# A four-mixer decoder trunk: the attention's value sum in fp32 products, and new constants for the planner that orders the instructions

## The chip, the cores and the metric

The kernel runs on one core of one Trainium2 chip. Time is the device time of one execution in microseconds, and each figure for a kernel is the median of its runs. A profile is one execution in which the hardware recorded every instruction; its span runs from the first instruction to the last.

## The reference

Two layers work on a sequence of 512 positions of width 1024, all in float32. Each layer does this:

```
h = rmsnorm(x);  z = h @ w_in                       # 1024 -> 13 column groups
y_a = a_b * conv3(a_c * a_h)                        # short causal convolution
y_b = g_u * (tril(W_s) @ layernorm(g_v) + b_s)      # per chunk of 128, 4 heads
y_c = attention(q, k, v), 4 heads of 64, rotary; of the admissible keys only the
      128 that score highest in sum_j w_idx_j * relu(q_idx_j . k_idx) take part
y_d = silu(layernorm(conv31(d_a * sigmoid(d_g)) + b))   # conformer, 31 taps
x = x + concat(y_a, y_b, y_c, y_d) @ w_out
x = x + (silu(hf @ w_gate) * (hf @ w_up)) @ w_down,  hf = rmsnorm(x)   # hidden 2816
```

A last rmsnorm closes the trunk.

## The kernel before

**Products.** Activations lie with features on the 128 partitions and the 512 positions along the free dimension. A product of two float32 matrices is made of three fp32r products: each operand is split into a high half, a copy rounded to fp32r (ScalarE, `pg.act`), and a low half, the operand less its high half (`pg.tt` with `subtract`, on VectorE or GpSimd); `mm3` then adds high times high, high times low and low times high in one bank of PSUM. A few small products (sums over partitions, spreading a row over partitions, transposes) use float32 operands directly, which here is called an fp32 product. In the trace an fp32 product shows as two records.

**Weights.** They come in units of 128 x 1024 in the order of use: 23 for the input projections of a layer (`in_units`, the order of whose parts is `ORDER`: c are the conformer's, a the attention's q and k, s the short convolution's, g the gate of the chunked mixer, z the values of both that mixer and the attention), 10 for the output projection, 44 for gate and up, 24 for down. `weights()` loads a unit and splits it; `POOL_LO` names the units whose low half GpSimd computes, `DEEP` those whose halves lie in the large pool of 68 buffers `u` of 128 x 512 (and whose load is gated) and not in the four `wh`/`wl` pairs. While layer 0's gate and up products run, all 33 input and output units of layer 1 are split and stored (`presplit`), and layer 1 loads them as pairs.

**Side chains.** Beside the projections run the rotary products (`rope`), the search for the 128 best keys (`topk`: 16 rounds of MAX8 and MATCH_REPLACE8 for each of three query blocks, on VectorE), the conformer's taps (`conf`: `TAPS` of the 31 on VectorE in a PSUM bank, the rest on ScalarE and GpSimd) and its layer norm (`conf_ln`), the softmax, and the value sum. The value sum, per head and per block `s_` of 128 keys: transposes of the probabilities into a bank `sm`, a split of that bank into `hi` and `lo`, and `mm3` with the halves `vh`, `vl` of the values into the bank `po`, over 512, 384, 256 and 128 columns.

**Output projection.** For each of its eight row blocks first the six groups `EARLY_K`, which are y[0], y[1], y[6], y[7], y[2], y[3], that is all but the attention; the attention's two (`LATE_K`) follow in a second pass.

**Order.** The program is first recorded as operations with their dependencies (`Program.add`). `order` then walks backwards for the latest time at which each may start (projection products, the mains, at nominal times stretched by `STRETCH`; other operations scaled by `HURRY`), subtracts the boost of its part (`BOOST`, one table a layer), and simulates the five engines forwards with a cost for each operation and a model of TensorE's clock (`clock`), always picking the most urgent operation that can start. The order that comes out is what each engine's queue holds. So the constants change no arithmetic, but they can move any instruction on its engine.

**Start.** `warm` puts `WARMUP` fp32 products of a constant at the head of TensorE's queue. The first unit (`HALVED`) is loaded and split in two halves.

## Time and profile before

| | |
|---|---|
| median of 3 runs | 1168.21 us (1168.18 to 1168.29) |
| profiled execution | 1167.96 us |
| its span | 1166.2 us |
| TensorE (PE) busy | 1146.0 us |
| VectorE (DVE) busy | 651.2 us |
| ScalarE (ACT) busy | 486.5 us |
| GpSimd (POOL) busy | 279.4 us |
| mean granted TensorE clock | 0.993 |

A matmul's record lasts longer than its share of the engine, because matmuls are pipelined: the engine's pace is read from the starts of consecutive records, or from a run in the chain of waits. A line number in a row is often that of a helper (L335 is `mm`, L383 `tt`, L392 `stt`, L429 and L431 `act`), so rows are told apart by the names of their tiles: `mm`, `cv`, `sm`, `po` are PSUM banks, `wr`, `wh`, `wl` a unit of weights and its halves, `u` everything in the large pool, `X` the residual stream. PE is TensorE, PEld its weight loads, DVE VectorE, ACT ScalarE, POOL GpSimd. The granted clock is a share of 2.4 GHz, and 0.50 is the lower level of 1.2 GHz.

### The profile page before, as it was taken

The page shows a single profiled execution, that of the slowest core. Times are in us where ns is not written, and L with a number is a line of the kernel's source. Part 1 is how long each engine was busy: PE and PEld are TensorE (multiplying, and loading weights), DVE is VectorE, ACT ScalarE, POOL GpSimd, SP SyncE. Part 2 cuts the span into 40 slices and gives each one's busy share as a digit, 9 for nine tenths or more (in the row PEclk, how much of TensorE's full clock was granted, in tenths as well). Part 3 has the DMA queues.
Part 4 walks back from the last instruction along what each step waited for, and adds up shares of the span by engine and source line. Part 5 has one row for each costly group of instructions (what it writes and reads, how often), then busy time and mean ns, then how long its engine had stood idle before and what let it go on. Part 6 is the DMA issues. An engine that isn't in the chain of part 4 may idle for free.

```text
span 1166.2 us, 14577 instructions
## 1 busy us (share of the span) xinstructions
PE 1146.0 (98%) x5266; PEld 934.1 (80%) x5266; DVE 651.2 (56%) x1169; ACT 486.5 (42%) x803; POOL 279.4 (24%) x213
## 2 busy tenths in 40 slices
PE   9999989999999999999999999999999999999996
PEld 6878768888888888888877787788888888888885
DVE  5799996644346566553236999756433433433212
ACT  7583557533234554442123553655323323332211
POOL 1758822211111111021111664003111111100111
PEclk9999989999999999999999999999999999999998
DMA  9620213232359999994672452232233232234202
GB/s 321 207 82 21 75 41 108 76 115 90 105 172 308 374 361 387 369 367 154 224 239 76 180 186 99 78 127 91 91 95 105 91 101 98 86 106 142 97 5 72
DMA packets 75576, 178.44 MB, mean 153 GB/s; under 512 B 9200, under 2 KB 15472, under 8 KB 75504
## 3 DMA queue, kind: packets, MB, share of 16 engines
q1 hardware_dynamic: 72304, 172.26, 42.8%
q10 hardware_dynamic: 3200, 5.25, 1.3%
q8 instruction: 41, 0.67, 0.2%
q14 instruction: 31, 0.25, 0.1%
HBM read 139.17 MB, written 34.11 MB: 149 GB/s over the span
## 4 chain that ended last, share of the span: by engine, by line
PE 82%; DVE 11%; DMA 2%; ACT 2%; issue 1%; POOL 0%; SPq 0%; DVEq 0%; POOLq 0%; ACTq 0%
PE mm L335 76%; DVE u L950 2%; DVE cv L392 2%; DVE u L383 2%; DVE m L949 2%; PE sm L352 2%; PE sm L335 1%; PE po L335 1%; DMA dr<-u 1%; DMA u<-w_dram 1%; DVE u L392 1%; ACT u L431 1%; PE cv L335 1%; PE sm L361 1%; DVE wl L383 1%
## 5 line engine op out<-in xcount | busy, mean ns | idle before, releaser
L335 PE MATMUL mm<-u,wh 128*128 128x512 f32 (+1 forms) x2548 | 735.9, 391 | 2.3 <-ACT wh L429 0.9
L335 PEld LDWEIGHTS mm<-u,wh 128*128 128x128 f32 (+1 forms) x2548 | 476.2, 187 | 105.0 <-DVE u L392 2.0
L335 PE MATMUL mm<-u,wl 128*128 128x512 f32 (+1 forms) x1274 | 432.3, 391 | 1.4 <-DVE wl L383 1.4
L383 POOL TENSOR_TENSOR u<-u,u 128x512 f32<-128x512 f32 (+10 forms) x174 | 237.5, 1376 | 754.0 <-ACT u L431 626.0
L429 ACT CAST wh<-wr 128x1024 fp32r<-128x1024 f32 (+2 forms) x151 | 152.6, 1016 | 375.2 <-PE mm L335 311.4
L335 PEld LDWEIGHTS mm<-u,wl 128*128 128x128 f32 (+1 forms) x1274 | 238.7, 187 | 52.2 <-DVE wl L383 3.1
L335 PE MATMUL mm<-u,u 128*128 128x512 f32 (+1 forms) x816 | 223.7, 380 | 0.3
L383 DVE TENSOR_TENSOR u<-mm,u 128x512 f32<-128x512 f32 x119 | 81.6, 689 | 232.0 <-PE mm L335 225.0
L383 DVE TENSOR_TENSOR wl<-wr,wh 128x1024 fp32r<-128x1024 f32 (+2 forms) x144 | 169.9, 1186 | 50.1 <-ACT wh L429 49.9
L335 PEld LDWEIGHTS mm<-u,u 128*128 128x128 f32 x816 | 147.6, 189 | 35.0 <-issue 4.2
L383 DVE TENSOR_TENSOR u<-u,u 128x512 fp32r<-128x512 f32 (+3 forms) x150 | 106.6, 734 | 32.6 <-ACT u L429 27.3
L429 ACT CAST u<-u 128x512 fp32r<-128x512 f32 (+2 forms) x148 | 84.6, 590 | 79.9 <-DVE u L383 26.5
L383 DVE TENSOR_TENSOR X<-X,mm 128x512 f32<-128x512 f32 (+1 forms) x49 | 32.9, 675 | 123.9 <-PE mm L335 123.9
L392 DVE SCALAR_TENSOR_TENSOR cv<-u,prm,cv 128x511 f32<-128x511 f32 (+17 forms) x72 | 52.8, 733 | 0.0
L950 DVE MATCH_REPLACE8 u<-m,u 128x256 f32<-128x256 f32 (+2 forms) x96 | 51.7, 541 | 0.0
L949 DVE MAX8 m<-u 128x8 f32<-128x512 f32 (+2 forms) x96 | 51.3, 550 | 0.3
L431 ACT ACTIVATE u<-u 128x512 f32<-128x512 f32 x60 | 37.8, 631 | 18.5 <-DVE u L383 15.5
L431 ACT ACTIVATE u<-X,prm 128x512 fp32r<-128x512 f32 (+1 forms) x39 | 27.4, 717 | 35.0 <-DVE X L383 34.6
L431 ACT ACTIVATE u<-u,prm 128x512 f32<-128x512 f32 (+13 forms) x56 | 35.2, 704 | 9.9 <-POOL u L383 8.8
L392 DVE SCALAR_TENSOR_TENSOR u<-X,prm,u 128x512 fp32r<-128x512 f32 x32 | 27.9, 904 | 11.4 <-ACT u L431 8.8
L431 ACT ACTIVATE u<-X 128x512 f32<-128x512 f32 (+1 forms) x33 | 19.8, 607 | 31.2 <-DVE X L383 27.8
L431 ACT ACT_TABLE_LOAD x18 | 23.1, 1283 | 22.2 <-DVE rc L660 9.8
(96 smaller groups left out, 501.0 us busy)
## 6 DMA issues: line engine op xcount, KB each, us to landing
wr<-w_dram SPq DMA_DIRECT2D x143, 512.0 KB, 3.6
dr<-u SPq DMA_DIRECT2D x114, 256.0 KB, 5.6
u<-w_dram SPq DMA_DIRECT2D x57, 256.0 KB, 5.7
u<-dr SPq DMA_DIRECT2D x56, 256.0 KB, 4.9
wr<-w_dram SPq DMA_DIRECT2D x24, 384.0 KB, 3.0
wh<-dr SPq DMA_DIRECT2D x12, 512.0 KB, 4.5
wl<-dr SPq DMA_DIRECT2D x12, 512.0 KB, 5.8
u<-u ACTq DMA_DIRECT2D x28, 128.0 KB, 2.3
```

The lines of the kernel that those rows point to most:

```text
L335: self.add("PE", cost, lambda: self.nc.tensor.matmul(out.ap(), l.ap(), r.ap(), start=start, stop=stop), [out.tile.view], [l, r], lat=0.2, ...
L352: self.nc.tensor.matmul(o.ap(), a.ap(), b.ap(), start=start, stop=stop)
L361: self.nc.tensor.transpose(o.ap(), x.ap(), ident.ap())
L383: self.add(eng, cost, lambda: self._e(eng).tensor_tensor(out=out.ap(), in0=a.ap(), in1=b.ap(), op=op), [out], [a, b], port=eng == "POOL" o ...
L392: self.add("DVE", 0.13 + 1.0417e-3 * out.n, lambda: self.nc.vector.scalar_tensor_tensor(out=out.ap(), in0=a.ap(), scalar=self._sc(s), in1= ...
L429: self.nc.scalar.copy(out.ap(), x.ap())
L431: self.nc.scalar.activation(out.ap(), x.ap(), func, **{k: self._sc(v) for k, v in kw.items()})
L949: pg.dve(n, lambda m8=m8, sc=sc: nc.vector.max(out=m8.ap(), in_=sc.ap()), [m8], [sc])
L950: pg.dve(n, lambda m8=m8, sc=sc: nc.vector.match_replace(out=sc.ap(), in_to_replace=m8.ap(), in_values=sc.ap(), imm_value=-3e38), [sc], [m8])
```

## The change

The value sum keeps values and probabilities as they are (`WHOLE`, both layers): one copy out of PSUM and one fp32 product a block, in place of a copy, a subtraction and three fp32r products. The conformer's tap counts are looked up by layer. The values of the constants of the order change: the order of the input parts (q1 and k1 ahead of gu1), stretch, boosts, clock model, the cost of a warm-up product and the number of them (12 to 17), the sets `DEEP` and `POOL_LO`, and a boost for the first half of a halved unit's split.

```diff
@@ -31,7 +31,7 @@
     "s0": [("ac", 0), ("ah", 0), ("ab", 0)], "s1": [("ac", 1), ("ah", 1), ("ab", 1)],
     "g0": [("gu", 0)], "g1": [("gu", 1)],
 }
-ORDER = ('z', 'c0', 'a0', 's0', 'c1', 's1', 'g0', 'g1', 'a1')
+ORDER = ('z', 'c0', 'a0', 's0', 'c1', 's1', 'g0', 'a1', 'g1')
 N_IN = 23
 COL = {"qi": QI, "q": Q, "k": K, "da": D_A, "dg": D_G, "ac": A_C, "ah": A_H, "ab": A_B, "gu": G_U}
 DOWN_PARTS = [(0, 8), (8, 16), (16, 22)]
@@ -200,7 +200,7 @@
                 o.key -= FIRST
 
         engs = ["PE", "DVE", "ACT", "POOL", "SP"]
-        self.slow, self.edge, self.busy = 2.0, WINDOW, 0.0
+        self.slow, self.edge, self.busy = 2.0, 2.3, 0.0
         free = dict.fromkeys(engs, 0.6)
         future = {e: [] for e in engs}
         avail = {e: [] for e in engs}
@@ -370,7 +370,7 @@
         def fn():
             for _ in range(n):
                 self.nc.tensor.matmul(out.ap(), x.ap(), x.ap(), start=True, stop=True)
-        self.add("PE", n * (1.667e-3 * out.n + 0.01), fn, [out], [x], lat=0.2)
+        self.add("PE", n * 0.185, fn, [out], [x], lat=0.2)
 
     def _sc(self, s):
         return s.ap() if isinstance(s, View) else s
@@ -465,23 +465,25 @@
 
 
 WINDOW, COOL, WARM = 3.41, 0.42, 0.7
-STRETCH = 1.18
-WARMUP = 12
+STRETCH = 1.09
+WARMUP = 17
 PRESPLIT = 3
+
+WHOLE = (0, 1)
 AHEAD = (80, 220)
-HURRY = 1.07
+HURRY = 1.19
 EARLY = -6.0
-FIRST = 104.0
+FIRST = 100.0
 FIN_POOL = (0, 2)
 
 BOOST = [
-    {"rope": -2.0, "conv": 19.0, "a": 16.0, "z": 6.0, "s": 30.0, "g": -2.0, "topk": 6.0, "att": 30.0, "out": -3.0},
-    {"rope": 2.0, "conv": 26.0, "a": -1.0, "z": -1.0, "s": 10.0, "g": -9.0, "topk": 2.0, "att": 20.0, "out": 6.0},
+    {"rope": -2.0, "conv": 19.0, "a": 16.0, "z": 4.0, "s": 15.0, "g": 4.0, "topk": 12.0, "att": 61.0, "out": -1.0},
+    {"rope": 2.0, "conv": 19.0, "a": -1.0, "z": 10.0, "s": 0.0, "g": 0.0, "topk": 3.0, "att": 2.0, "out": -1.0},
 ]
-DEEP = (2, 4, 5, 6, 7, 9, 10, 11, 12, 13, 15, 20, 23, 25, 26, 28)
+DEEP = (4, 5, 6, 7, 9, 10, 11, 12, 15, 20, 23, 25, 31)
 HALVED = (0,)
-TAPS = (18, 20)
-POOL_LO = (5, 7, 10, 11, 12, 14, 18, 20, 21, 22, 23, 29, 31, 32)
+TAPS = (18, 20, 18, 20)
+POOL_LO = (3, 5, 7, 11, 12, 14, 20, 21, 22, 23, 25, 26, 29, 31)
 
 
 def build(tc, nc, a, o):
@@ -592,7 +594,9 @@
             hi, lo = (pg.tile(t, [128, 1024], F32R)[:, :w] for t in ("wh", "wl"))
             for n, c in enumerate((slice(0, w // 2), slice(w // 2, w))):
                 first_load(raw[:, c], a["w"][i, :, c], 2 + 6 * n)
+                pg.boost += 20.0 * (1 - n)
                 split(raw[:, c], hi[:, c], lo[:, c])
+                pg.boost -= 20.0 * (1 - n)
             return lambda c, n: (hi[:, c:c + n], lo[:, c:c + n])
         sooner = pg.mains[-AHEAD[0]:][:1] if i >= N_UNITS + N_IN + N_OUT else ()
         pg.dma(raw, a["w"][i, :, :w], after=gate if deep else sooner)
@@ -780,7 +784,7 @@
             pg.tt(ar, pa, R, ALU.mult)
             pg.tt(yp, ar, gr, ALU.mult, "POOL")
             w = [pm[:, P_WC + CW * i + d:P_WC + CW * i + d + 1] for d in range(CW)][::-1]
-            cv, cd, nv = pg.tile("cv", [128, S]), U(), TAPS[i]
+            cv, cd, nv = pg.tile("cv", [128, S]), U(), TAPS[2 * l + i]
             pg.act(cv, yp, AF.Identity, scale=w[0], bias=pm[:, P_BC + i:P_BC + i + 1])
             for e in range(1, nv):
                 pg.stt(cv[:, e:], yp[:, :S - e], w[e], cv[:, e:], ALU.mult, ALU.add)
@@ -842,14 +846,17 @@
             gv, vn = [], []
             for t in range(4):
                 if t % 2 == 0:
-                    g2, h2, l2 = U(), U(F32R), U(F32R)
+                    g2, h2 = U(), U(F32 if l in WHOLE else F32R)
+                    l2 = h2 if l in WHOLE else U(F32R)
                 c = slice(256 * (t % 2), 256 * (t % 2) + 256)
                 gv.append(g2[:, c])
                 vh.append(h2[:, c])
                 vl.append(l2[:, c])
                 pg.act(gv[t], pz[t][:, :G])
                 pg.act(vh[t], pz[t][:, G:], AF.Copy, scale=rs[:, t:t + 1])
-                pg.stt(vl[t], pz[t][:, G:], rs[:, t:t + 1], f(vh[t]), ALU.mult, ALU.subtract)
+                if l not in WHOLE:
+                    pg.stt(vl[t], pz[t][:, G:], rs[:, t:t + 1], f(vh[t]), ALU.mult,
+                           ALU.subtract)
 
 
             ws, bl, lbs, wsh, wsl = U(), U(), U(F32R), U(F32R), U(F32R)
@@ -991,6 +998,15 @@
                 pt = SM()[:, :n]
                 pg.trs([pt[:, 128 * (b - s_):128 * (b - s_) + 128] for b in range(s_, 4)],
                        [probs[h, b][:, 128 * s_:128 * s_ + 128] for b in range(s_, 4)], ident)
+                if l in WHOLE:
+                    if s_ < 3:
+                        hi = U()
+                        pts[s_] = hi[:, :n]
+                        if s_ == 1:
+                            pts[3] = hi[:, 384:]
+                    pg.act(pts[s_], pt)
+                    pg.mm(po[:, 128 * s_:], vh[s_][:, c], pts[s_], s_ == 0, s_ == 3)
+                    continue
                 if s_ < 3:
                     hi, lo = U(F32R), U(F32R)
                     pts[s_] = hi[:, :n], lo[:, :n]
```

## Rows read from the trace of the kernel before

**Rows 1.** The page's busy line: us, share of the span, instructions.

```profile
PE 1146.0 (98%) x5266; PEld 934.1 (80%) x5266; DVE 651.2 (56%) x1169; ACT 486.5 (42%) x803; POOL 279.4 (24%) x213
```

**Rows 2.** Stretches: us, busy PE, PEld, DVE, ACT, POOL, clock, DMA share, GB/s.

```profile
0.00:25.00 25.00, 22.56 (x95) 16.50 (x96) 11.02 (x18) 19.16 (x39) 3.62 (x11) 1.00 0.93 338
...
143.00:152.00 9.00, 8.03 (x38) 6.26 (x37) 9.00 (x24) 3.89 (x7) 8.27 (x6) 1.00 0.24 73
152.00:165.00 13.00, 9.51 (x37) 6.84 (x38) 12.73 (x34) 10.44 (x19) 0.55 (x1) 0.74 0.09 31
...
178.00:205.00 27.00, 27.00 (x163) 22.47 (x161) 16.10 (x46) 19.36 (x49) 6.62 (x3) 1.00 0.34 115
...
660.00:719.00 59.00, 58.03 (x262) 46.67 (x260) 57.70 (x134) 22.84 (x42) 34.95 (x32) 1.00 0.53 191
...
775.00:800.00 25.00, 24.54 (x108) 19.94 (x108) 19.41 (x23) 13.41 (x20) 8.95 (x6) 1.00 0.14 46
...
1150.00:1166.00 16.00, 6.07 (x42) 5.30 (x40) 6.55 (x23) 3.55 (x9) 2.82 (x4) 0.71 0.39 131
```

**Rows 3.** Timeline of TensorE, 140 to 206 us: start, us, instruction, idle before it.

```profile
151.17 0.62 PE L335 MATMUL mm<-u,wh 128*128 128x512 f32 x2
155.06 1.16 PE L335 MATMUL sm<-ident,rs 128*128 128x128 f32 x8 [3.26 <-DVE rs L392]
...
157.13 0.80 PE L335 MATMUL mm<-u,wl 128*128 128x512 f32 x1 [0.43 <-DVE wl L383]
```

**Rows 4.** One microsecond of the stretch from 152 to 165, columns as in rows 2.

```profile
157.00:158.00 1.00, 0.87 (x2) 0.78 (x3) 1.00 (x3) 0.29 (x1) 0.00 (x0) 0.50 0.00 0
```

**Rows 5.** The chain that ended last, in order of time: start, us, what.

```profile
25.90 0.89 PE sm L335 x8
...
203.01 1.85 PE po L335 x12
204.87 23.49 PE mm L335 x103
```

**Rows 6.** Timeline of TensorE around the two fp32 products of 512 columns.

```profile
141.50 1.02 PE L335 MATMUL sm<-u,o 128*128 128x512 f32 x2
142.29 0.93 PE L335 MATMUL mm<-u,u 128*128 128x512 f32 x3
...
713.37 1.13 PE L335 MATMUL sm<-u,o 128*128 128x512 f32 x2 [0.59 <-POOL u L383]
...
714.57 0.39 PE L335 MATMUL mm<-u,u 128*128 128x512 f32 x1
```

**Rows 7.** VectorE's groups by shape: count, busy us, mean ns, idle before.

```profile
L383 DVE TENSOR_TENSOR u<-sm,u 128x512 fp32r<-128x512 f32 x8 | 5.2, 687 | 1.5 <-ACT u L429 1.4
...
L383 DVE TENSOR_TENSOR u<-sm,u 128x384 fp32r<-128x384 f32 x8 | 4.3, 547 | 0.2 <-ACT u L429 0.2
...
L383 DVE TENSOR_TENSOR u<-sm,u 128x256 fp32r<-128x256 f32 x8 | 3.4, 419 | 3.3 <-ACT u L429 3.3
...
L392 DVE SCALAR_TENSOR_TENSOR u<-mm,rs,u 128x256 fp32r<-128x256 f32 x6 | 2.7, 480 | 0.5 <-ACT u L429 0.3
...
L383 DVE TENSOR_TENSOR u<-sm,u 128x128 fp32r<-128x128 f32 x8 | 1.9, 281 | 1.0 <-ACT u L429 1.0
```

**Rows 8.** Groups by shape: a unit's low half on VectorE and on GpSimd.

```profile
L383 DVE TENSOR_TENSOR wl<-wr,wh 128x1024 fp32r<-128x1024 f32 x123 | 150.4, 1228 | 19.9 <-ACT wh L429 19.8
...
L383 POOL TENSOR_TENSOR wl<-wr,wh 128x1024 fp32r<-128x1024 f32 x6 | 14.4, 2402 | 16.8 <-ACT wh L429 16.8
```

**Rows 9.** Timeline of VectorE, 196 to 232 us.

```profile
205.52 0.69 DVE L383 TENSOR_TENSOR u<-po,u 64x512 fp32r<-64x512 f32 x1 [3.07 <-ACT u L429]
...
212.45 0.69 DVE L383 TENSOR_TENSOR X<-X,mm 128x512 f32<-128x512 f32 x1 [0.27 <-PE mm L335]
```

**Rows 10.** Timeline of TensorE in the first microseconds.

```profile
1.06 5.49 PE L372 MATMUL mm<-ones 128*128 128x128 f32 x24 [1.06 <-POOL ones L631]
...
7.40 0.73 PE L335 MATMUL mm<-u,wh 128*128 128x512 f32 x2 [0.86 <-ACT wh L429]
```

## Prediction

> **What bounds the kernel now.** I read the page's busy line first. TensorE is busy for 1146.0 of 1166.2 us, VectorE for 651.2 [rows 1]. So a column more on TensorE is paid in full, and all that can be won is TensorE's idle time and slow clock. The idle time is 1166.2 - 1146.0 = 20.2 us, and the stretches say where. The first 25 us hold 25.00 - 22.56 = 2.4 us, the stretch from 1150 to the end 16.2 - 6.07 = 10.1, and neither is in the part that is rewritten, except for the warm-up. That leaves 7.7 us in the middle [rows 1, 2].
>
> Of these, 9.00 - 8.03 = 1.0 and 13.00 - 9.51 = 3.5 us lie between 143 and 165 us, in layer 0's mixers, and there alone the mean granted clock is under 1: 0.74 over 13 us, which is (1 - 0.74) x 13 = 3.4 us of work lost [rows 2]. The timeline shows the event. TensorE starts its last two ready products at 151.17, then idles 3.26 us until VectorE delivers `rs`, the conformer's layer norm scale, at 155.06, and waits once more for a weight's low half from VectorE at 157.13 [rows 3]. After that gap the clock stands at the lower level, 0.50 of full, 1.2 GHz, through the microsecond at 157 and beyond [rows 4]. This one stall costs 1.0 + 3.5 + 3.4 = 7.9 us. The other 7.7 - 4.5 = 3.2 us of idle time are spread; layer 1's counterpart holds 59.00 - 58.03 = 1.0, its entry into the FFN 0.5 [rows 2].
>
> The cause is a queue on VectorE. It is busy 9.00 of 9.00 us before the stall and 12.73 of 13.00 in it [rows 2]: top-k, conformer taps, rotary products and weight splits share it, and TensorE has used up the input projections before the conformer's output exists (the first output unit needs y[6], y[7] as its third and fourth products).
>
> **The change part by part.** *The value sum on TensorE.* Today a head takes twelve fp32r products, and a run of twelve takes 1.85 us [rows 5]. Afterwards it takes four fp32 products over 512 + 384 + 256 + 128 = 1280 columns. Their price is read from fp32 products that are already there. Four of 128 columns (eight records, so two a product) take 0.89 us, 1.74 ns a column [rows 5]. One of 512 columns (two records) starts at 141.50 and the next work at 142.29, 0.79 us; the other starts at 713.37, and after it and one fp32r product (23.49 / 103 = 0.23 us) it is 714.57, so 0.97 [rows 5, 6]. Per column these are 1.54 and 1.89 ns. A head then costs 1280 x 1.74 = 2.22 us (1.97 to 2.42), that is 0.37 more than 1.85 (0.12 to 0.57), and eight heads cost **+2.9 us** (+1.0 to +4.6). I take the middle, because the run of four is the one most like the new sum.
>
> The section "Back-to-back issue gap" of the Trainium skill's page "TensorE: Matmul & The Clock Gate" gives one gap for N columns at full clock, N / 2.4 GHz + 2.5 ns, and makes no exception for fp32. By it a head's four products would take about 0.54 us, an estimate from that page, and the term would be a gain of some 10 us in place of the loss. The eight records of the four small fp32 products contradict it: 0.89 us where the page's gap gives 0.22.
>
> *The splits on VectorE.* The subtractions that make the low halves of the probabilities go: 32 of them, 5.2 + 4.3 + 3.4 + 1.9 = 14.8 us. So do eight of the values' low halves at 0.48, 3.8 us [rows 7]. ScalarE's copies stay, since the high half was a copy of the same shape. So 18.6 us leave an engine that is off the path for most of the span, and only what is queued ahead of something TensorE waits for counts. The 7.4 us a layer of the probabilities fall in the value sums, 178 to 205 us, where VectorE is busy for 16.10 of 27 and TensorE never idle [rows 2]: nothing directly. The values' 1.9 us a layer come before top-k. One wait also goes (a product no longer waits for a subtraction, and the bank of transposes comes free earlier); output products cover it today, so I count nothing; without that cover each block would give back its subtraction, 0.28 to 0.69 us.
>
> *Splits that change engine.* In layer 0, units 10 (k0), 18 (ab1) and 32 go from GpSimd to VectorE, units 3 (z0), 25 and 26 the other way. A 1024-wide one costs 1.23 us on VectorE and 2.40 on GpSimd [rows 8]. Two of those that come to VectorE fall before the stall, +2.4 us against the 1.9 that the values free. In amount, then, VectorE's queue there is not shorter. If the stall goes, it goes by order.
>
> *The order.* What can be moved is top-k and attention. The last value sum's split ends at 205.52 + 0.69 = 206.2, and the first late output group, six products of 0.23 us, ends at 212.45, so starts near 211.1: attention has 4.9 us to spare [rows 5, 9]. The removed subtractions give it up to 7.4 us more. So top-k can make way for the conformer by about ten microseconds, more than the 3.3 + 0.4 us by which the conformer is late [rows 3]. Moving q1 and k1 ahead of gu1 also starts the last two heads one unit sooner. The boosts speak both ways: layer 0's `s` falls from 30 to 15, behind `conv` at 19, but `topk` rises from 6 to 12 and `att` from 30 to 61. `HURRY` rises, which draws long side chains forward, and the conformer's is one. I take most of the stall as gone, with 1.7 us left of 7.9, a little over what layer 1's counterpart still loses: **-6.2** (bounds -7.9 and 0). For the 3.2 us elsewhere, with 9.3 us less on VectorE in each layer, I take **-1.3** (-3.2 to 0).
>
> *The start.* Twelve warm-up products take 5.49 us, 0.46 each, and end at 6.55; the first real product starts at 7.40 [rows 10]. Five more end at about 8.9 at that pace, and at 7.7 at the full-clock 0.22 of the 128-wide fp32 product [rows 5]; so first work slips 0.3 to 1.5 us. Unit z0's low half comes 2.40 - 1.23 = 1.2 us later from GpSimd [rows 8], with unit qi1 now loaded without its gate to fill in. Later waits for data in these 25 us absorb part (2.4 us idle [rows 2]). I take **+0.5** (-0.6, if the earlier first split starts TensorE sooner and hides the rest, to +2.7).
>
> *At nothing.* The tap counts are the same 18 and 20 for both layers. The deep set changes which buffers hold four units' halves; the splits stay as wide in sum and products cover them. Layer 1's input and output weights come split from memory as before; if a pair came late, a wait like the 0.5 us one would appear. The gate, up and down products are untouched, and that stretch has no idle time worth a term.
>
> **Sum.** The profiled execution took 1167.96 us (span 1166.2, 1.8 outside), 0.25 below the median of 1168.21. 1167.96 + 2.9 - 6.2 - 1.3 + 0.5 = 1163.9, and with the 0.25 added, **1164**.
>
> **The rivals.** (A) As above, 0.44: own range 1160.5 to 1165.8.
>
> (B) Every stall goes, as VectorE's queue is shorter and better ordered: 1168.2 + 2.9 - 7.9 - 3.2 = 1160.0. For it: the slack above. Against: VectorE stays full ahead of the stall. 0.13.
>
> (C) The other side. The conformer stays late: two more splits and a top-k that has moved nearer to it keep VectorE's queue as long, TensorE again runs dry near 151 us, and the clock falls again. The price is the unhidden 2.9 of fp32, 0.5 at the start, -1.3 elsewhere: 1168.2 + 2.1 = 1170.3, or 1171.6 with nothing won elsewhere. It decides from the point where less than about 2.9 of the 11.1 us of stalls and slow clock goes. 0.19.
>
> (D) The stall is shortened, not removed: idle without the fall of the clock, or half of it. About 3.4 of 7.9 saved: 1168.2 + 2.9 + 0.5 - 3.4 = 1168.2. 0.17.
>
> (E) The new order makes a second stall of that kind, at the value sums, where TensorE now waits on ScalarE's copies, or in layer 1: 1168.2 + 2.1 + 7.9 = 1178.2. Today's 27.00 of 27.00 busy there [rows 2] speaks against it. 0.05.
>
> (F) An fp32 product costs no more than an fp32r one. A head would take a third of 1.85, eight heads -9.9 in place of +2.9, and the time 1151.3. This is the skill's rule above; the two records a product and 0.89 us [rows 5] speak against it. 0.02.
>
> **How the numbers follow.** About 0.2%, 2.3 us, is what a measurement of this kernel can tell from no change. Faster: A, B and F, 0.59; no change: D, 0.17; slower: C and E, 0.24. The range for 8 in 10 runs from B's low side, 1159, to C's high side, 1171.5; it leaves out E, F and the edges of B and C.
>
> **What would show it.** In the new trace: two long records a product in the value sum, a run of four over 1280 columns at 2.2 us (2.0 to 2.4); no low-half subtraction reading `sm` or scaled by `rs` on VectorE, some 18 us less of its time; TensorE's idle time in the middle down from 7.7 us to about 3, its clock at full through 143 to 165 us; TensorE's time in value sums up by about 3. The prediction is wrong if the clock still falls in layer 0, if the fall only moves to another stage, or if the fp32 sum costs more than 4.6 us because fp32 and fp32r products alternate badly. Then the order, not the arithmetic, is what I misjudged.

## The result, and the profile after

The changed kernel takes 1179.57 us (median of 4 runs, 1177.65 to 1180.32), the kernel before 1168.25 beside it (1168.18 to 1169.81). The ratio is 1.0091, 95% interval 1.0078 to 1.0105: slower by 0.9%. Forecast were 1164.0 us and a range that ended at 1171.5.

The page of the changed kernel (span 1178.5 us, profiled run 1180.32), the line that answers to [rows 1]:

```profile
PE 1149.3 (98%) x5244; PEld 931.1 (79%) x5244; DVE 640.9 (54%) x1125; ACT 484.8 (41%) x798; POOL 272.1 (23%) x214
```

TensorE is busy 3.3 us longer and idle 1178.5 - 1149.3 = 29.2 us in place of 20.2. So most of the loss is waiting. VectorE's busy time is 10.3 us shorter, not 18.6. The low halves of [rows 7] are all gone; what came back is mostly in other splits: there are three more of 1024 columns, and those of 512 take 0.80 us in the mean in place of 0.74.

Stretches of the changed kernel, columns as in [rows 2]:

```profile
0.00:25.00 25.00, 22.18 (x104) 16.65 (x105) 9.85 (x17) 19.40 (x39) 3.96 (x12) 1.00 0.95 340
...
125.00:150.00 25.00, 21.65 (x92) 16.78 (x92) 24.97 (x50) 7.76 (x14) 21.07 (x17) 1.00 0.23 69
150.00:175.00 25.00, 21.63 (x103) 16.39 (x103) 22.29 (x53) 14.25 (x25) 8.16 (x6) 1.00 0.15 49
...
200.00:225.00 25.00, 22.44 (x99) 14.66 (x98) 10.14 (x29) 15.35 (x39) 0.36 (x1) 0.93 0.12 41
...
450.00:475.00 25.00, 22.14 (x91) 17.84 (x90) 13.48 (x19) 11.43 (x17) 3.81 (x3) 0.93 1.02 380
```

The slow clock of [rows 2] and [rows 4] is gone from the stage around 155 us, but it shows in two others, each (1 - 0.93) x 25 = 1.75 us, together 3.5 us, about the 3.4 of before. The idle time, too, lies in more places than it did. The list of what TensorE waited for up to 240 us, so in layer 0's mixers, says how: total us, times, longest us. First the kernel before:

```profile
PE sm L335 <- DVE rs L392: 3.3, 1, 3.3
PE mm L335 <- DVE wl L383: 1.4, 3, 0.8
PE mm L372 <- POOL ones L631: 1.1, 1, 1.1
PE mm L335 <- ACT wh L429: 0.9, 1, 0.9
```

Then the changed kernel:

```profile
PE mm L335 <- DVE wl L383: 3.4, 4, 2.1
PE sm L352 <- DVE u L383: 1.8, 1, 1.8
PE sm L335 <- DVE rs L392: 1.4, 1, 1.4
PE sm L335 <- POOL u L383: 1.2, 1, 1.2
PE mm L335 <- DVE u L383: 1.2, 2, 0.7
PE sm L352 <- DVE mx L403: 1.2, 1, 1.2
PE mm L372 <- POOL ones L635: 1.1, 1, 1.1
PE mm L335 <- ACT u L429: 1.0, 2, 0.7
PE mm L335 <- ACT wh L429: 1.0, 1, 1.0
PE po L335 <- DVE u L383: 0.6, 1, 0.6
PE mm L335 <- DVE u L392: 0.6, 2, 0.3
```

The wait for `rs` did shrink, from 3.3 to 1.4 us. But the sum of the list went from 6.7 to 14.5 us, and in place of six waits it holds seventeen. And one wait came far from there, at 469 us in layer 0's FFN (the feed-forward part: the gate, up and down products). TensorE's timeline of the changed kernel (start, us, instruction, idle before it), around the longest of them:

```profile
57.74 0.73 PE L352 MATMUL sm<-u,u 64*128 64x512 f32 x4 [1.84 <-DVE u L383]
...
149.80 0.50 PE L335 MATMUL mm<-u,wl 128*128 128x512 f32 x1 [2.10 <-DVE wl L383]
...
155.59 1.13 PE L335 MATMUL sm<-ident,rs 128*128 128x128 f32 x8 [1.38 <-DVE rs L392]
...
205.59 0.55 PE L352 MATMUL sm<-u,u 64*128 64x128 f32 x5 [1.16 <-DVE mx L403]
...
465.95 0.39 PE L335 MATMUL mm<-u,wl 128*128 128x512 f32 x1
469.20 0.73 PE L335 MATMUL mm<-u,wh 128*128 128x512 f32 x2 [2.86 <-DVE u L383]
```

Where the time went along the span shows best on TensorE's own work. The program has 4722 projection products in the same number in every kernel here, so I compare the starts of the product with 864 before it (the mixers of layer 0 and its output projection are done), of that with 2160 before it (layer 0's FFN has run on past 469 us), of that with 3312 before it (layer 1's mixers are done), and the end of the span. They are counted from the traces, in us later than in the kernel before:

```
                              865th   2161st   3313th     end
after                        +10.34   +14.36   +12.01  +12.27
fp32_old_order                +1.22    +0.74    -0.26   -0.29
new_order_fp32r               +6.69   +11.89    +9.27   +9.37
old_constants_fp32            +9.63   +10.24    +9.42   +9.35
new_constants_split          +11.41   +13.82   +24.61  +24.93
half_search                   +9.20   +11.62    +9.30   +9.52
pool_halves_new               +8.02   +10.43    +9.18   +9.41
one_store                    +12.28   +16.28   +14.26  +14.46
ffn_eviction_moved            +8.12    +8.47    +6.97   +7.37
waits_moved                   +4.16    +4.35    +1.87   +2.09
half_searches_new             +3.09    +7.11    +4.47   +4.71
stall_moved                   +1.52    +1.95    +2.05   +2.02
half_searches_old             -0.98    -0.71    -0.72   -0.74
chain_moved                   +0.86    +1.77    +1.84   +1.64
chain_and_lows_moved          +5.62    +6.24    +6.44   +5.92
```

So the change loses 10.3 us in layer 0's mixers and 4.0 more in its FFN, and wins 14.36 - 12.01 = 2.35 in layer 1. These are one profiled execution each, and a median can stand some 2 us off it. The table itself shows that: *ffn_eviction_moved* changes nothing ahead of the FFN, and yet its 865th product stands at +8.12 and not at +10.34. Most of the difference is the wait of 1.84 us at 57.74, which it does not have.

Two causes can be read from rows. **A queue.** In the FFN the bank that TensorE wants is evicted by VectorE (`u<-mm`). VectorE's timeline, then ScalarE's:

```profile
467.22 1.23 DVE L383 TENSOR_TENSOR wl<-wr,wh 128x1024 fp32r<-128x1024 f32 x1 [1.71 <-ACT wh L429]
468.37 1.28 DVE L383 TENSOR_TENSOR u<-mm,u 128x512 f32<-128x512 f32 x2
```

```profile
466.15 1.04 ACT L429 CAST wh<-wr 128x1024 fp32r<-128x1024 f32 x1 [1.36 <-PE mm L335]
```

The eviction stands behind the split of a weight that TensorE does not need yet (with the split put behind it, below, the wait shrinks to 0.5 us). That split waits for a cast, and the cast waits for a buffer that TensorE's last products before the stall give back. A free engine, a finished product, and 2.86 us of waiting. **A lock.** VectorE's subtraction of two operands in SBUF, the engines' working memory, takes 1.23 us at 128x1024 [rows 8], and 0.66 at 128x512 where nothing delays it (below). VectorE's timeline of the changed kernel has longer ones:

```profile
54.85 2.84 DVE L383 TENSOR_TENSOR u<-u,u 128x512 fp32r<-128x512 f32 x1
...
147.24 0.54 DVE L957 MATCH_REPLACE8 u<-m,u 128x384 f32<-128x384 f32 x1
147.70 2.05 DVE L383 TENSOR_TENSOR wl<-wr,wh 128x1024 fp32r<-128x1024 f32 x1
```

and GpSimd's has, at those times:

```profile
54.78 2.36 POOL L383 TENSOR_TENSOR wl<-wr,wh 128x1024 fp32r<-128x1024 f32 x1 [3.29 <-ACT wh L429]
...
147.40 1.27 POOL L383 TENSOR_TENSOR u<-u,u 128x512 f32<-128x512 f32 x1 [0.68 <-ACT u L431]
```

In each pair VectorE's instruction outlasts GpSimd's by less than its own length: GpSimd ends at 54.78 + 2.36 = 57.14 and VectorE at 57.69; GpSimd at 148.67 and VectorE at 149.75. TensorE's waits of 1.84 and 2.10 us end within 0.05 us of that. The search step ahead of the second, at 147.24, ran into the same GpSimd instruction and kept its length. That VectorE and GpSimd lock each other out of a shared port pair for a whole instruction, when VectorE reads two SBUF operands, stands in the Trainium skill, "SBUF — State Buffer", section "SBUF: two separate sides"; these rows agree, 2.84 us for 0.66.

Which of the two starts first is not the order's to say. In *ffn_eviction_moved*, whose order up to there is the same to the instruction, the subtraction of 54.85 started before GpSimd's, and TensorE did not wait. VectorE's row, then GpSimd's:

```profile
54.28 0.66 DVE L387 TENSOR_TENSOR u<-u,u 128x512 fp32r<-128x512 f32 x1
```

```profile
54.73 2.47 POOL L387 TENSOR_TENSOR wl<-wr,wh 128x1024 fp32r<-128x1024 f32 x1 [2.23 <-ACT wh L433]
```

Of the six profiled runs with this order there, GpSimd was first in the changed kernel and in *one_store*, and only these two have the wait of 1.8 us.

### The profile page after: what moved, and what is told of

Same layout as the page of the kernel before. It is cut to its first block, busy times and chain, and to the rows that moved or that the text cites. A ratio compares the mean times of both kernels' runs of the same rounds, so it can differ in the third digit from the quotient of the medians.

```text
span 1178.5 us, 14460 instructions
## 1 busy us (share of the span) xinstructions
PE 1149.3 (98%) x5244; PEld 931.1 (79%) x5244; DVE 640.9 (54%) x1125; ACT 484.8 (41%) x798; POOL 272.1 (23%) x214
## 4 chain that ended last, share of the span: by engine, by line
PE 82%; DVE 11%; DMA 2%; ACT 2%; issue 1%; ACTq 0%; POOL 0%; DVEq 0%
PE mm L335 77%; DVE cv L392 3%; DVE u L383 2%; DVE u L957 2%; DVE m L956 2%; PE po L335 2%; PE sm L352 2%; PE sm L335 1%; ACT u L431 1%; PE sm L361 1%; DVE wl L383 1%; DMA u<-u 1%; DVE u L392 1%; DMA wr<-w_dram 1%; DMA X<-x_dram 1%
## 5 line engine op out<-in xcount | busy, mean ns | idle before, releaser
L335 PE MATMUL mm<-u,wh 128*128 128x512 f32 x2628 | 801.1, 392 | 4.9 <-DVE u L383 3.3
L335 PEld LDWEIGHTS mm<-u,wh 128*128 128x128 f32 x2628 | 491.0, 188 | 112.4 <-issue 5.9
L335 PE MATMUL mm<-u,wl 128*128 128x512 f32 x1314 | 488.3, 392 | 3.6 <-DVE wl L383 3.6
L383 POOL TENSOR_TENSOR u<-u,u 128x512 f32<-128x512 f32 (+12 forms) x174 | 229.7, 1332 | 797.4 <-ACT u L431 650.6
L335 PEld LDWEIGHTS mm<-u,wl 128*128 128x128 f32 x1314 | 246.1, 187 | 57.6 <-DVE wl L383 5.8
L335 PE MATMUL mm<-u,u 128*128 128x512 f32 (+1 forms) x696 | 183.1, 373 | 2.2 <-DVE u L383 1.2
L335 PEld LDWEIGHTS mm<-u,u 128*128 128x128 f32 x696 | 125.3, 188 | 28.3 <-DVE u L383 2.2
L383 DVE TENSOR_TENSOR u<-u,u 128x512 fp32r<-128x512 f32 (+2 forms) x150 | 109.6, 747 | 53.2 <-ACT u L429 32.0
L429 ACT CAST u<-u 128x512 fp32r<-128x512 f32 (+1 forms) x148 | 84.9, 590 | 81.8 <-DMA u<-w_dram 31.1
L957 DVE MATCH_REPLACE8 u<-m,u 128x512 f32<-128x512 f32 (+2 forms) x96 | 51.7, 541 | 0.0
L431 ACT ACTIVATE u<-u,prm 128x512 f32<-128x512 f32 (+13 forms) x56 | 34.9, 699 | 11.3 <-POOL u L383 11.2
```

The costliest lines, as they stand in the source:

```text
L335: self.add("PE", cost, lambda: self.nc.tensor.matmul(out.ap(), l.ap(), r.ap(), start=start, stop=stop), [out.tile.view], [l, r], lat=0.2, ...
L383: self.add(eng, cost, lambda: self._e(eng).tensor_tensor(out=out.ap(), in0=a.ap(), in1=b.ap(), op=op), [out], [a, b], port=eng == "POOL" o ...
L429: self.nc.scalar.copy(out.ap(), x.ap())
L431: self.nc.scalar.activation(out.ap(), x.ap(), func, **{k: self._sc(v) for k, v in kw.items()})
L957: pg.dve(n, lambda m8=m8, sc=sc: nc.vector.match_replace(out=sc.ap(), in_to_replace=m8.ap(), in_values=sc.ap(), imm_value=-3e38), [sc], [m8])
```

## Experiments

### Arithmetic and order apart

*fp32_old_order*: the old order to the instruction, with the new sums. The two dropped products and the low halves keep their place in the order and issue nothing.

```diff
+    def sum3(out, lh, rh, first, last):
+        (ah, al), (bh, bl) = lh, rh
+        for n, (x, y_) in enumerate(((ah, bh), (ah, bl), (al, bh))):
+            pg.mm(out, x, y_, first, last)
+            pg.ops[-1].cost = max(0.1, 0.4167e-3 * y_.n + 0.0133)
+            if n:
+                pg.ops[-1].fn = lambda: None
...
-                mm3(po[:, 128 * s_:], (vh[s_][:, c], vl[s_][:, c]), pts[s_], s_ == 0, s_ == 3)
+                pg.ops[-1].fn = lambda: None
+                sum3(po[:, 128 * s_:], (vh[s_][:, c], vl[s_][:, c]), pts[s_], s_ == 0, s_ == 3)
```

> The kernel before with its exact order on every engine; only the value sum is done in fp32 products of unsplit probabilities and values, and the subtractions for their low halves are not issued. Theory O (the loss is in the new order; the arithmetic costs what the small fp32 products showed, 0.37 us a head): 1171 us (1169 to 1172.5), layer 0's attention ends within 2 us of where it ended before (206.2). Theory F (the fp32 products themselves cost far more, by alternating with fp32r products): 1177 or more.

Measured: 1167.9 us (before 1168.38), ratio 0.9996 [0.9987, 1.0006]. That is under Theory O's range by 1 us, and 9 under Theory F's.

*new_order_fp32r*: the new order to the instruction, each fp32 product issued as three fp32r products of the high halves. The low halves are left out.

```diff
-                    pg.mm(po[:, 128 * s_:], vh[s_][:, c], pts[s_], s_ == 0, s_ == 3)
+                    thrice(po[:, 128 * s_:], vh[s_][:, c], pts[s_], s_ == 0, s_ == 3)
```

> The changed kernel with its exact order; each fp32 product of the value sum is replaced by three fp32r products of the high halves (the low halves are left out), no subtraction. Theory O: only the 2.9 us of the arithmetic come back, 1176.5 us (1175 to 1178.5), and layer 0 still falls 8 us or more behind. Theory F: most of the 11 us come back, 1170 or less.

Measured: 1175.95, ratio 1.0062 [1.0047, 1.0077]: Theory O's range, though layer 0 is behind by 6.7 us and not by 8.

*old_constants_fp32*: the new arithmetic, planned anew with all of before's constants and cost figures. Against the kernel before, beside the lines of the new value sum:

```diff
+WHOLE = (0, 1)
...
-TAPS = (18, 20)
+TAPS = (18, 20, 18, 20)
```

> The changed kernel's arithmetic with all constants of the kernel before (order of parts, boosts, sets, stretch, clock and warm-up model), planned anew. Theory O, in the form that the constants are at fault: 1173 or less, with layer 0's search for the best keys ended by 175 us and its attention by 212. Theory O in the form that any change of costs makes the planner's order fall out by several us either way: anywhere from 1168 to 1180, with a new place of the stall. Theory F: 1178 or more.

Measured: 1176.99, ratio 1.0072 [1.0057, 1.0087]: not the 1173 or less of constants at fault, but inside the range of the second form.

*new_constants_split*: the new constants, planned for the old arithmetic (`WHOLE = ()`).

> The changed kernel with the split value sum of the kernel before (three fp32r products, low halves computed), planned anew with the new constants. Theory O, constants at fault: 1177 or more, layer 0 behind by 8 us or more. Theory F: 1170 or less.

Measured: 1193.34, ratio 1.0217 [1.02, 1.0234]. Here 10.8 us of the loss arise in layer 1, by the table.

The first two answer the main question. The arithmetic in the old order costs nothing that can be measured. The new order without the arithmetic is slower by 0.6%. The other two say what kind of thing the order is: neither set of constants is good in itself, since before's constants are as bad for the new arithmetic as the new constants are, and the new constants are much worse for the old arithmetic. A planner that lists some seven thousand instructions by due time gave another order after each of these edits, and the one of before is the best of the four. Why it is, no run shows. Nor was any one constant or set (`DEEP`, `POOL_LO`, the warm-up) put back by itself.

### Three suspects for the new order

*half_search*: in the new order the search of the second query block, which now ends at 192.3 in place of 170.1 us, does 8 of its 16 rounds.

```diff
+                if (l, b) == (0, 1) and rnd >= 8:
+                    for o_ in pg.ops[-2:]:
+                        o_.fn = lambda: None
```

> The changed kernel with its exact order, but layer 0's search for the second query block (256 wide) does 8 of its 16 rounds; the other 8 are left out, some 7 us of VectorE. Theory S (the late search holds back layer 0's attention and that holds back TensorE after 202 us): the search ends near 181 in place of 192.3, the last value sum's split near 211 in place of 221.2, and the time falls by 5 us or more (1174 or less). Rival V (the value sums on TensorE are themselves the chain there): attention ends within 2 us of 221 and the time stays within 2 us of 1179.6.

Measured: 1179.05, ratio 1.0078 [1.0054, 1.0103]. The search ends at 177.3, and the last value sum at 218.8, where it had ended at 219.9. So Rival V: this search's late end is not what holds attention back.

*pool_halves_new* and *pool_halves_old*: GpSimd's wide two-operand instructions issued in two halves, so that the lock is shorter, in the new and in the old order.

```diff
...
+        if eng == "POOL" and out.shadow.ndim == 2 and out.n >= 480:
+            h = out.n // 2
+            parts = [(out[:, c], a[:, c], b[:, c]) for c in (slice(0, h), slice(h, out.n))]
...
```

> The changed kernel with its exact order; GpSimd's tensor operations of 480 columns and more are issued as two halves, so that a colliding VectorE instruction can get in between. Theory K (VectorE loses 16 us up to 165 us, in place of 8 before, to instructions that stand still while GpSimd reads SBUF, and this makes the conformer and the search late): that loss falls by a third or more, layer 0 gains 3 us or more, time 1176.5 or less. Rival (only the order of the queue counts): 1179 or more, as GpSimd gets slower by the second fixed cost.

> The kernel before with its exact order and the same halves on GpSimd. Theory K: less is to be won, 0 to 2 us (1166 to 1168.5). Rival: 1169 or more from GpSimd's longer work.

Measured: 1177.32, ratio 1.0062 [1.0042, 1.0082], and 1169.32, ratio 1.0005 [0.999, 1.002]. In the new order that lies between Theory K (1176.5 or less) and its rival (1179 or more), and its interval just overlaps that of the changed kernel. By the traces, what VectorE's instructions took beyond the median length of their shape in the same run, up to 165 us, is 8.6 us before, 16.1 in the changed kernel and 10.4 with the halves. But its 865th product, at +8.02, is no earlier than the +8.12 of *ffn_eviction_moved*, where GpSimd's instructions are whole. That the collisions cost TensorE up to 2 us is possible, then, but not shown; they are not the whole loss.

*one_store*: of layer 1's stored weights only the high halves are written and read (for both halves), so half the stores to memory in layer 0's FFN.

> The changed kernel with its exact order, but of layer 1's stored weights only the high halves are written, and they are read for both halves (the low halves are left out): a third less traffic while layer 0's gate and up products run. Theory D (the new stall of 2.9 us near 466 us and the slow clock after it come from late transfers): that stall goes, time 1175.5 (1174.5 to 1176.5). Rival Q (it comes from the order of the evictions and splits on VectorE): it stays, 1179 or more.

Measured: 1180.75, ratio 1.0085 [1.0056, 1.0113]. The stores to memory between 240 and 475 us went from 86 to 43 (and what was moved in all from 57.4 to 46.3 MB, a fifth less), but the list of TensorE's waits from 440 to 480 us still has:

```profile
PE mm L335 <- DVE u L383: 2.9, 1, 2.9
```

Late transfers are not its cause: Theory Q.

### The waits of the new order moved away

*ffn_eviction_moved*: the two evictions go ahead of the split that stood in front of them on VectorE. The moves name instructions by their place in the program; each goes right behind the second.

```diff
-        for o in self.order():
-            o.fn()
+        seq = [o.i for o in self.order()]
+        for x, y in MOVES:
+            seq.remove(x)
+            seq.insert(seq.index(y) + 1, x)
+        for i in seq:
+            self.ops[i].fn()
...
+MOVES = ((3126, 2223), (3186, 3185))
```

> The changed kernel as it is, but for two evictions of projection banks in layer 0's feed-forward part, which go ahead of one cast on ScalarE and one weight split on VectorE. Nothing is left out. Theory H (that stall of 2.86 us is a matter of who stands first in a queue: the eviction was ready and waited behind a split that waited for a cast that waited for TensorE): the wait falls under 1 us and the slower clock after it goes: 1175.5 to 1177.5 us. Rival D (the weights come late over the DMA queues, so that the wait returns at the next block): 1179 to 1180.

*waits_moved*: eight pairs more, for the long waits of layer 0.

```diff
+MOVES = ((149, 759), (898, 1139), (899, 898), (901, 899), (1019, 901), (911, 910), (1013, 913), (1631, 1236), (3126, 2223), (3186, 3185))
```

> The changed kernel with the two evictions moved as in the run beside it, and six more moves in layer 0, one for each of TensorE's longer waits there: a low-half subtraction of the first scores goes right behind a weight split (wait 1.84 us), five projection products go ahead of the conformer's statistics product that waits for GpSimd (1.25 us), a weight split goes ahead of top-k work (2.10 us), the square behind the square root goes ahead of a cast and the two instructions that end in rs go ahead of a multiply-add (1.38 us), and a weight split goes behind two row maxima (1.16 us). Nothing is left out. Theory H (layer 0's loss is these waits, each made by one instruction that stands ahead of the one that TensorE needs): 5 to 6 us of layer 0's 10.3 come back, with the feed-forward's 2 to 4: 1170 to 1173 us. Rival G (one wait's end is the next one's start, VectorE being late through the whole stage): at most 2 us of layer 0's come back, 1174 to 1178.

Measured: 1175.46, ratio 1.0064 [1.0044, 1.0084], and 1171.39, ratio 1.0024 [1.0013, 1.0034]. With the two evictions alone the wait of 2.86 us shrinks to 0.5, and the granted clock is 1.00 from 440 to 480 us. The ten pairs shift eight of the 7369 planned instructions by one to five places in their engine's queue, and by the medians that takes back 8.2 of the 11.3 us. Theory H holds in the main: most of the new order's loss is instructions that stand a few places too far back. In layer 0's mixers the moves give 4.0 us beside *ffn_eviction_moved* (+8.12 to +4.16), not the 5 to 6 expected, since the wait of 1.84 us was not the order's. Of the waits that were left, TensorE's timeline has these among others:

```profile
145.57 0.50 PE L339 MATMUL mm<-u,wl 128*128 128x512 f32 x1 [1.31 <-DVE wl L387]
...
150.73 1.13 PE L339 MATMUL sm<-ident,rs 128*128 128x128 f32 x8 [0.74 <-DVE rs L396]
```

### Could the old order's stall have been taken away?

My forecast said so. Here is that step alone, in the old order.

*stall_moved*: the last links of the chain to `rs`, and what TensorE needs next, go ahead of what stood before them.

```diff
+MOVES = ((918, 917), (919, 918), (1361, 919), (702, 1361), (920, 702), (921, 920), (1364, 1363), (1365, 1364), (1366, 1365), (1367, 1366))
```

> The kernel before, old arithmetic and old order, but for ten places of that order: on ScalarE the square root of the layer-0 normalisation and the square behind it go ahead of a cast; on VectorE the two instructions that end in rs go ahead of eight others (top-k, low-half subtractions), and the split that makes the next low half of the weights goes right behind the reciprocal; on TensorE four projection products that need that low half go ahead of the products that wait for rs. Nothing is left out. Theory M (the forecast's price of the stall was right, only the new order did not take it away): TensorE's 3.26 us wait falls to about 1 us, so 2.2 us, and the half-clock spell behind it goes too, 3.4 us: 1162.6 to 1166 us, about 1163.5. Theory G (the waiting is given back: VectorE is what is late there, and the wait comes again within twenty us): 1167.5 to 1169.

Measured: 1169.34, ratio 1.0008 [0.9999, 1.0017]. That is Theory G, 0.3 us above its range. TensorE's timeline has no wait for `rs` any more, but:

```profile
153.15 0.51 PE L339 MATMUL mm<-u,wl 128*128 128x512 f32 x1 [1.22 <-DVE wl L387]
...
158.33 0.44 PE L356 MATMUL sm<-u,u 64*128 64x128 f32 x4 [2.84 <-DVE u L387]
159.62 1.76 PE L356 MATMUL sm<-u,u 64*128 64x512 f32 x6 [0.85 <-DVE u L387]
```

The 3.26 + 0.43 of [rows 3] became 1.22 + 2.84 + 0.85: the low halves of the scores, which were second in line, are late now.

*moved_and_layer1_fp32*: the same, with fp32 value sums in layer 1 alone.

> The kernel before with the ten moves of the first run, and in layer 1 alone the value sums as single fp32 products, with the low-half subtractions of the values and of the probabilities not issued there. Nothing is left out of the result. Layer 1 gained 1.0 us by that arithmetic in the old order's own run, layer 0 lost 1.2. Theory M: 0.5 to 1.0 us under the first run, about 1162.7. Theory G: 1166.5 to 1168.

Measured: 1169.09, ratio 1.0004 [0.9994, 1.0015]: above both ranges, nearer to Theory G's.

*half_searches_old* and *half_searches_new*: amount in place of order. All searches of layer 0 do 8 of 16 rounds.

```diff
+                if l == 0 and rnd >= 8:
+                    for o_ in pg.ops[-2:]:
+                        o_.fn = lambda: None
```

> The kernel before in its own order and arithmetic, but all three searches of layer 0 do 8 of their 16 rounds (the other rounds are left out, so the choice of keys in layer 0 is another). That takes some 25 us of work from VectorE between 94 and 170 us and changes no other instruction's place. Theory Q (the stall before rs is one of amount: VectorE has more to do ahead of the conformer's layer norm than the time allows): the waits of 3.26 and 0.43 us and the half-clock spell go: 1160.5 to 1163.5 us. Theory L (it is one of hand-offs: conformer output, GpSimd's square, TensorE's sums, VectorE, a table load on ScalarE, VectorE again, whatever else is queued): the wait falls by no more than about 1 us and the clock still falls: 1166 to 1168.5.

> The changed kernel in its own order, with the same rounds of layer 0's searches left out. Theory Q: 5 us or more of layer 0's 10.3 come back: 1174.5 us or less. Theory L (the new waits there are hand-offs and instructions that stand still behind GpSimd's, which the searches do not set): 1176.5 to 1180.

Measured: 1166.96, ratio 0.9983 [0.9971, 0.9996], and 1174.23, ratio 1.0047 [1.003, 1.0063]. In the old order VectorE's busy time between 94 and 170 us fell from 74.43 to 59.39, and yet the wait and the clock stayed. The old order with half the searches, TensorE's timeline and the stretch from 152 to 165 us:

```profile
154.50 1.20 PE L335 MATMUL sm<-ident,rs 128*128 128x128 f32 x8 [2.59 <-DVE rs L392]
```

```profile
152.00:165.00 13.00, 10.45 (x41) 7.65 (x42) 8.79 (x20) 9.94 (x18) 0.35 (x1) 0.74 0.09 30
```

VectorE is now busy for 8.79 of 13 us, and TensorE still waits 2.59. So it is not a full queue (my forecast's "The cause is a queue on VectorE"), but mostly a chain of hand-offs. It begins with TensorE's sums at 149.46; the timelines of VectorE and ScalarE have the rest:

```profile
151.12 0.18 DVE L660 RECIPROCAL rc<-sm 128x4 f32<-128x4 f32 x1
...
154.30 0.15 DVE L392 SCALAR_TENSOR_TENSOR rs<-tt,sm 128x4 f32<-128x4 f32 x1
```

```profile
151.87 1.28 ACT L431 ACT_TABLE_LOAD   x1
```

In the new order the same cut gives 5.3 us back, which meets Theory Q's range. But it also takes out search steps that stood in front of a weight split there, so it does not part amount from order: *waits_moved* shortened the wait for that split from 2.10 to 1.31 us with the searches whole.

*chain_moved*: the chain from its start, GpSimd's sum of squares, 39 moves between 143 and 162 us. *chain_moved_layer1_fp32*: with layer 1's sums in fp32.

> The kernel before, old arithmetic, with the whole chain of hand-offs behind the conformer moved earlier, not only its last link: on GpSimd the sum of the two squares goes one place ahead, on TensorE the four products that add it up go ahead of fourteen projection products, on VectorE and ScalarE the steps to rs follow at once, the low halves of scores and of weights that TensorE needs next go ahead of five search steps, and those go behind. 39 places in all between 143 and 162 us. Nothing is left out. Theory L (the stall is a chain of hand-offs that starts too late; VectorE's amount is not short): no wait over 1 us is left between 150 and 162 us and the half-clock spell goes or is halved: 1161 to 1165 us, which would be faster than both kernels. Theory G (whatever is moved ahead there, something else is late by as much): 1167 to 1169.

> The same moves, and layer 1's value sums as single fp32 products without low halves, as in the earlier run of that kind. Nothing is left out of the result. Theory L: 0.5 to 1 us under the run beside it, 1160.5 to 1164.5. Theory G: 1166.5 to 1168.5.

Measured: 1168.81, ratio 1.0002 [0.9992, 1.0011], and 1167.78, ratio 0.9999 [0.999, 1.0008]. Theory G in both. No wait for `rs` is left. In *chain_moved*, the timeline of TensorE and the stretch:

```profile
156.10 0.44 PE L356 MATMUL sm<-u,u 64*128 64x128 f32 x4 [1.16 <-DVE u L387]
157.39 1.76 PE L356 MATMUL sm<-u,u 64*128 64x512 f32 x6 [0.85 <-DVE u L387]
```

```profile
152.00:165.00 13.00, 10.86 (x43) 8.12 (x44) 12.81 (x31) 9.19 (x16) 1.49 (x1) 0.74 0.09 31
```

*chain_and_lows_moved* and *chain_and_lows_layer1_fp32*: those low halves go ahead as well, in place of three search steps.

> As the run that moved the whole chain, old arithmetic, but the low halves of scores that TensorE waited for there (1.16 and 0.85 us) go on VectorE ahead of the chain's steps, in place of three more search steps, which go behind the score rows. Nothing is left out. Theory L: no wait over 0.6 us is left between 150 and 162 us, the clock stays at the higher level through the stage, and what shows is the stall's whole price: 3.5 to 7 us under before, 1161.5 to 1165. Theory G (the searches that make way end later and the wait comes at the value sums, or the next hand-off is late by as much): 1167.5 to 1170.

> The same order, and layer 1's value sums as single fp32 products without low halves. Nothing is left out of the result. Theory L: 0.5 to 1 us under the run beside it. Theory G: 1167 to 1169.5.

Measured: 1174.09, ratio 1.0048 [1.0033, 1.0062], and 1172.85, ratio 1.0043 [1.0029, 1.0056]. Worse than either theory had it. TensorE's timeline of *chain_and_lows_moved*, then VectorE's:

```profile
154.27 0.73 PE L339 MATMUL mm<-u,wh 128*128 128x512 f32 x2 [2.14 <-DVE u L387]
...
161.12 4.94 PE L339 MATMUL mm<-u,u 128*128 128x512 f32 x19 [1.05 <-DVE u L387]
...
171.48 0.50 PE L339 MATMUL mm<-u,u 128*128 128x512 f32 x1 [4.06 <-DVE X L387]
```

```profile
148.75 3.12 DVE L387 TENSOR_TENSOR u<-u,u 128x512 f32<-128x512 f32 x2
...
170.76 0.67 DVE L387 TENSOR_TENSOR X<-X,mm 128x512 f32<-128x512 f32 x1
```

The new waits are of kinds seen above. The two subtractions moved to 148.75 take 3.12 us where GpSimd is busy (143.67 to 151.33); the search steps that had stood there kept their length. And the search steps put off now stand before an output eviction, `X`, which comes 4.06 us late.

## Why the prediction was wrong

**The step that failed** is "The order", the term of -6.2 us for layer 0's stall, with its sentences "If the stall goes, it goes by order" and "So top-k can make way for the conformer by about ten microseconds". Top-k made way in part (the second block's search ends 22 us later, at 192.3; the other two end some 20 us earlier, at 147.8 and 145.5), and the wait for `rs` shrank by 1.9 us. But layer 0's mixers got 10.3 us longer (8.1 in another execution of the same order), of which four heads' fp32 products are 1.2. Two faults lie in the step. First, it priced the stall as idle time plus slow clock, and took both as gone with the wait. It named nothing that is late next. Three orders by hand show what is: a weight's low half, the scores' low halves, an output eviction. From 150 to 172 us TensorE's waits come to 5.3, 3.3 and 7.3 us there, in place of the 3.26 + 0.43 of [rows 3]. And the clock fell in all three (0.76, 0.74 and 0.87 over the stretch from 152 to 165 us, 0.74 in [rows 2]). In the changed kernel it does hold through that stretch, and falls at 207 and at 470 us instead: one of the forecast's own signs of being wrong, "if the fall only moves to another stage". Second, it read the cause as VectorE's full queue, because VectorE was busy 12.73 of 13.00 us [rows 2]. With 15 us of that work gone the wait was still 2.59. A busy engine beside a wait is not yet its cause; the chain to `rs` goes from TensorE to VectorE, ScalarE and VectorE again.

**Not foreseen:** the FFN. "The gate, up and down products are untouched, and that stretch has no idle time worth a term": the products are untouched, but the order of the evictions and splits beside them is not, and 4.0 us were lost there (2.4 of idle time, 1.7 of slow clock). Two moved evictions took them back (from +10.34 / +14.36 to +8.12 / +8.47 in the table).

**Splits that change engine:** "In amount, then, VectorE's queue there is not shorter" was right and not enough. I counted the length of each and not whom it stops: a split on GpSimd holds up VectorE (2.84 us for 0.66), and one on VectorE is held up by GpSimd (2.05 for 1.23). How much of TensorE's loss that is stays open, as the run with GpSimd's instructions in halves is not clear of the noise.

**The value sum: right.** The new chain's rows, start, us, what:

```profile
213.85 2.25 PE po L335 x8
...
774.82 2.16 PE po L335 x8
```

2.16 to 2.25 us a head, forecast 2.22, against 1.85 [rows 5]: 2.5 to 3.2 us for eight heads, forecast 2.9. (Two more such runs read 2.43 and 2.36, but the starts of their first and last records lie as close together, 2.15 us against 2.12 and 2.05.) In the old order the layer-0 half shows as +1.2, and layer 1 gives 1.0 back. There two waits for ScalarE, 1.0 us together, are gone from TensorE's list; that it is the missing subtractions that ended them is likely, but not shown. That a true fp32 product takes four passes stands in the Trainium skill, "FP8 and Floating Point Precision", section "TensorE Precision Notes"; rows agree with it (at 512 columns two records, 0.43 us from start to start, where an fp32r product takes 0.23), and rival F is dead. The formula N / 2.4 GHz + 2.5 ns, which the prediction took from the Trainium skill, "TensorE: Matmul & The Clock Gate", section "Back-to-back issue gap", stands there for an isolated product. The 0.23 us between fp32r products agrees with its 0.216 for 512 columns, an estimate from that page; the fp32 products do not.

**The start:** +0.5 forecast; the first real product now starts earlier than in [rows 10], by the same timeline of the changed kernel:

```profile
6.99 0.71 PE L335 MATMUL mm<-u,wh 128*128 128x512 f32 x2
```

but the first 25 us hold 22.56 - 22.18 = 0.4 us more idle time, and the 101st projection product starts at 34.43 us in place of 33.92. So +0.5 fits.

**Elsewhere:** -1.3 forecast for both layers; layer 1 alone gives 2.35 (1.3 to 2.6 in the other runs of this order, by the table), with its four heads' fp32 price in it. More than I took.

**The rivals.** E, "a second stall of that kind", priced 1178.2 and given 0.05, comes nearest, but that its price fits is luck: it stood for one more stall like the old one, with the old one still there, and what came were many short waits in layer 0's mixers, a smaller one for `rs`, and one in the FFN, while layer 1 got faster. Its kind, a new order with new waits, had too small a chance: I took TensorE's 27.00 of 27.00 in the value sums as a sign of slack, while it only says that this one order, planned with the old costs, had no hole there. Of C, waits near 151 us came (2.10 us until 149.80, 1.38 until 155.59), without the fall of the clock there. Of the eight orders run here that are not the old one (three planned, five with moves), none was faster than it by what can be measured. The forecast gave no weight to that.

**Open:** layer 0's last 4.2 us in *waits_moved* were not taken apart: 2.9 are idle time (9.83 us up to the 865th product, 6.98 before), and the rest is about the 1.2 of four fp32 heads. But the 3.4 us of slow clock of before are gone there too, so as much of TensorE's busy time has no account (the five more warm-up products are 0.7 of it). Whether any order removes the old stall was not settled: three did not. No version that does the whole work beat both kernels; the nearest are the fp32 sums in the old order, 0.9996, and *chain_moved_layer1_fp32*, 0.9999.

## What to carry to other kernels

Where a planner makes the order from costs, an edit to the costs is two edits: measure the arithmetic in the old order first, and judge the new order by itself. Price a stall only after naming what is late next on the same engine, and check whether the chain behind it or the engine's amount sets it: where a cut of the suspected load leaves the wait standing, the load was not its cause. Look at a wait in several executions before you call it the order's: one of 1.84 us here came in two of six. When a split or a subtraction changes place between VectorE and GpSimd, count whom it stops, not only how long it takes.

## What the runs showed of the hardware

VectorE's instructions with two SBUF operands stood still beside GpSimd's: 2.84 us for 0.66, 2.05 for 1.23, 3.12 for two of 0.66. Its search steps did not: in *chain_and_lows_moved* one of 384 columns took 0.53 at 147.96, with GpSimd busy from 143.67 to 151.33, and one took 0.54 at 165.89, with GpSimd idle. So search steps are what to leave beside a busy GpSimd, which the last two runs did not do.

The slow clock cost as much as before and moved. Before, it was one fall in layer 0; after, two falls of half the size, behind waits of 1.16 us (with one of 0.60 a microsecond later) and of 2.86 us; in *waits_moved* the granted clock is 1.00 over 0 to 165, 165 to 235 and 440 to 480 us, where the longest wait left is 1.31 us. The length of the wait alone does not decide it. The same wait of 2.86 us, in the same order, has a fall with it or just behind it in the changed kernel, *one_store*, *new_order_fp32r* and *half_searches_new*, and none in *half_search* and *pool_halves_new*, whose granted clock is 1.00 from 440 to 480 us. What decides it was not tried.
